# An FFN down-projection on one core: its first group's raw weights in buffers of another tag, and its residual loads ahead of the second group's operands

## The chip, the core and the metric

The kernel runs on one core of one Trainium2 chip. The metric is the device time of an execution in microseconds (us). PE is TensorE, DVE is VectorE, ACT is ScalarE, POOL is GpSimd; SP is the sync engine, which does nothing here but issue DMAs. GpSimd issues DMAs too, from a queue of its own.

## What is computed

One layer of a hybrid encoder, in float32, for two sequences of 512 tokens (called s0 and s1 in the kernel) of width 1024. Cut to what matters here:

```python
def encoder_layer(h, p, ...):
    ...                                   # pooling mixer and attention
    h = h + jnp.concatenate([y_pool, y_att], axis=-1) @ w_o
    u2 = rms_norm(h, ln2)
    h = h + (jax.nn.silu(u2 @ w_gate) * (u2 @ w_up)) @ w_down      # 1024 -> 2816 -> 1024
    gate = jax.nn.sigmoid(rms_norm(h, ple_norm) @ w_ple_gate)
    return h + gate * (p @ w_ple_proj)                             # p: 256 wide
```

## The kernel before, in words

Every product of matrices is made of three TensorE products: each operand is split into a high and a low part (L128 on ACT makes the high part, L131 on DVE the low one), and high x high, high x low and low x high are summed (L155 to L157).

**Seven products for eight.** From the FFN on, a block of two by two tiles is computed by a scheme of the Strassen-Winograd kind, in `seven` (L679 on): seven products where eight would be plain. Their moving operands are B11, B21, T1, T2, T4, T3, B22 (blocks of the activations, or sums of them); the block's rows are two feature tiles, its columns the two sequences. Each of the seven has its own stationary operand, which the generator `stationary` makes out of two raw weight tiles: three parts are pieces of the raw tiles, four are totals s1 to s4 (L641 on DVE), and all are split into high and low. These weights come from a ring W of 8 buffers, so they are made up to eight products ahead. The raw tiles are read by `load` (L139 to L142) from SP's queue into tag R, which has two buffers of 1024 columns. The product T2 is accumulated onto the PSUM bank of the product B11 after that has been read, T3 onto the same bank, and B22 onto the bank of T1.

**FFN up.** Eleven steps (two feature tiles each) make gate and up, then silu(gate) * up, and the seven operands of the down-projection. `spill` (L842 to L846) splits each and writes it to DRAM from SP's queue, through buffers `st` of tag V or, except in the last step, A.

**FFN down.** The 22 feature tiles are taken in groups of `DOWN = (2, 3, 3, 3)` pairs. A group reads its 7 n operand tiles (n is 2 or 3, 512 KB each) back from DRAM (L917, GpSimd's queue), into buffers whose tags come from the list `free`: TAGS of the seven names before (L723: PT, QK, A, A, A, QK, A). Then it runs four sevens (m = 0, 2, 4, 6 in L918 on), one per pair of output tiles; each is 7 x n x 3 matmuls of 128x512. Each product is added to the residual h by DVE in `got` (L929), eight additions a seven. Raw weight tiles of the first group have 512 columns (256 KB), those of the others 768.

**The residual h** has been saved to DRAM (hsave0 for s0, hsave1 for s1) before the FFN. It is read again in `h_again` (L890 to L894), two tiles of 512 KB (one of each sequence) ahead of each of the first group's four sevens, from GpSimd's queue: by `"VA"[q is s0]` s0's go into tag A and s1's into V. V has four buffers, which the last step's spills use until their DMAs have landed.

**After the down-projection** come the embedding products (e, `embed`, L942 on, from pT and w_pp, loaded by `embedding_operands` into tag A in the middle of the last group), a norm, and the last gate.

The order of the instructions on each engine is set by a scheduler from dependences and the order in which the program is written; buffers of a tag rotate, and whoever takes one waits until its last user is done. SP and GpSimd issue strictly in order, so a DMA that waits holds up all behind it. Buffers by tag: A 20, QK 8, V 4, PT 4, W 8, R 2, F 12 (of 512 columns, used for the FFN's intermediate x tiles), G 4.

Of the kernel before, what the change touches and what calls it, by code (L numbers as in the profile page):

```python
# [11 lines left out]
F32 = mybir.dt.float32  # L12
# [5 lines left out]
P = 128  # L18
T = 512
NT = T // P  # L20
D = 1024
KD = D // P
# [14 lines left out]
DOWN = (2, 3, 3, 3)  # L37
# [49 lines left out]
def hybrid_layer(ctx: ExitStack, tc: tile.TileContext, a: dict, out: bass.AP):  # L87
    nc = tc.nc
# [5 lines left out]
    def nm(s):  # L94
        serial[0] += 1
        return f"{s}{serial[0]}"

    def sbuf(s, tag, shape, dt):
        return pool.tile([P] + shape, dt, tag=tag, name=nm(s), bufs=BUFS[tag])

    def At(s, tag="A", dt=F32R):
        return sbuf(s, tag, [2, T], dt)

    def Ft(s):
        return sbuf(s, "F", [T], F32)
# [6 lines left out]
    def eng(name, i=0):  # L112

        return nc.gpsimd if TURNS[name][i % len(TURNS[name])] == "p" else nc.vector
# [10 lines left out]
    def split(hi, lo, src, hi_eng="act", lo_eng=nc.vector):  # L125

        if hi_eng == "act":
            nc.scalar.activation(hi, src, AF.Copy)  # L128
        else:
            nc.vector.tensor_copy(hi, src)  # L130
        lo_eng.tensor_tensor(lo, src, hi.bitcast(F32), op=ALU.subtract)  # L131
# [5 lines left out]
                                       op0=ALU.mult, op1=ALU.subtract)  # L137

    def load(src, n=D, tag="R"):  # L139
        raw = sbuf("raw", tag, [D], F32)  # L140
        nc.sync.dma_start(raw[:, :n], src)
        return raw  # L142

    def weight(src, n=D, tag="W", hi="act", lo=None, raw_tag="R"):
        raw = load(src, n, raw_tag)
        if lo is None:
            turn[1] += 1
            lo = eng(phase[0], turn[1])
        w = [sbuf("wh", tag, [D], F32R), sbuf("wl", tag, [D], F32R)]
        split(w[0][:, :n], w[1][:, :n], raw[:, :n], hi, lo)  # L150
        return w
# [76 lines left out]
    def square_sum(acc, x, first, eng):  # L228
        if first:
            nc.scalar.activation(acc, x, AF.Square)  # L230
        else:
            sq = Ft("sq")
            nc.scalar.activation(sq, x, AF.Square)
            eng.tensor_tensor(acc, acc, sq, op=ALU.add)
# [5 lines left out]
    seqs = [Seq(), Seq()]  # L240
    s0, s1 = seqs
# [125 lines left out]
    def pooling():  # L367
        for q in seqs:
            q.yp = []
            q.ypt = [At("yp", dt=F32) for _ in range(NG // 2)]  # L370
        raw = load(a["w_pool"], NG * P)
        wp = (sbuf("wp", "F", [T], F32R), sbuf("wp", "F", [T], F32R))
        split(wp[0], wp[1], raw[:, :NG * P], lo_eng=nc.gpsimd)
# [215 lines left out]
    def output(q, htag, bank):  # L589
        while len(q.ys) < KD:  # L590
            mixed(q, len(q.ys))
            if len(q.ys) % 4 == 0:
                yield
        q.h, q.hp = [], []
        q.sq = Ft("sqh")
        for m in range(KD):
            w = weight(a["w_o"][m])
            if m % 2 == 0:
                hp = At("h", htag, F32)
                nc.sync.dma_start(hp, a["xT"][q.s, :, m:m + 2, :])  # L600
                q.hp.append(hp)
            ps = Ps("o", bank)
            for i, (k, y) in enumerate(q.ys):
                mm3(ps, cols(w, k * P), act(y), i == 0, i == KD - 1)
                if i == KD // 2 - 1:
                    yield
            hm = hp[:, m % 2, :]
            nc.vector.tensor_tensor(hm, hm, ps, op=ALU.add)
            q.h.append(hm)
            square_sum(q.sq, hm, m == 0, eng("sqh", m))  # L610
            yield
# [14 lines left out]
        e.tensor_tensor(d, x, y, op=ALU.subtract)  # L626
        return d

    def stationary(srcs, n, part):


        half = n * P

        def parts(x, k):
            w = sbuf("w", "W", [2, T], F32R)
            split(w[:, 0, :half], w[:, 1, :half], x, lo_eng=eng("wlo", k))
            return w

        def total(x, y, op, k):
            d = sbuf("s", "G", [T], F32)[:, :half]  # L640
            eng("wadd", k).tensor_tensor(d, x, y, op=op)  # L641
            return d

        raw = load(srcs[0], 2 * half)
        a11, a12 = raw[:, :half], raw[:, half:2 * half]
        if part != 1:
            yield parts(a11, 0)
            yield parts(a12, 1)
        if part == 0:
            return  # L650
        raw = load(srcs[1], 2 * half)
        a21, a22 = raw[:, :half], raw[:, half:2 * half]
        s1 = total(a21, a22, ALU.add, 0)
        yield parts(s1, 2)
        s2 = total(s1, a11, ALU.subtract, 1)
        yield parts(s2, 3)
        yield parts(a22, 6)
        s3 = total(a11, a21, ALU.subtract, 3)
        yield parts(s3, 5)
        s4 = total(a12, s2, ALU.subtract, 2)  # L660
        yield parts(s4, 4)

    AHEAD = BUFS["W"]
    made, jobs = [], []
# [14 lines left out]
    def seven(u, n, got, a_tag=None, tags=(None,)):  # L679


        def product(ps, b, first):
            w = made.pop(0)
            for j in range(n):
                mm3(ps, (w[:, 0, j * P:(j + 1) * P], w[:, 1, j * P:(j + 1) * P]), act(b[j]), first and j == 0, j == n - 1,
                    not first)
            fill()
            return ps

        def bank(name):  # L690
            t = tags[turn[0] % len(tags)]
            if t is not None:
                turn[0] += 1
            return Ps(name, t)

        a = product(Ps("a", a_tag), u["B11"], True)
        got(0, a)
        got(1, product(bank("c"), u["B21"], True))
        yield
        b = product(bank("b"), u["T1"], True)  # L700
        got(2, b)
        got(3, product(a, u["T2"], False))
        got(4, product(bank("d"), u["T4"], True))
        got(5, product(a, u["T3"], False))
        got(6, product(b, u["B22"], False))
# [17 lines left out]
    TAGS = {"B11": "PT", "B21": "QK", "T1": "A", "T2": "A", "B22": "A", "T4": "QK", "T3": "A"}  # L723
# [11 lines left out]
    HALF = KD // 2  # L735
# [32 lines left out]
    def run(*gens):  # L768
        for g in gens:
            for _ in g:  # L770
                pass
# [14 lines left out]
    s0, s1 = seqs  # L786
# [29 lines left out]
    last = output(s1, "V", None)  # L816
    steps(last, 10)
    u = {}
# [8 lines left out]
    f0 = 0  # L827
    for n in DOWN:
        f1 = f0 + 2 * n
        jobs += [([a["w_down"][m + i, :, f0 * P:f1 * P] for i in range(2)], n, None) for m in range(0, KD, 2)]  # L830
        f0 = f1
    jobs += [(w, HALF, 0) for w in pg] + [(w, HALF, 1) for w in pg]
    fill()
# [5 lines left out]
    hsave = [[dram.tile([P, 2, T], F32, name=f"hsave{s}p{j}") for j in range(HALF)] for s in range(2)]  # L839
# [46 lines left out]
    for gg, gu in pairs:  # L886
        run(started.pop(0) if started else seven(u, HALF, gg))
        run(started.pop(0) if started else seven(u, HALF, gu))

    def h_again(j):  # L890
        for q in seqs:
            hp = At("h", "VA"[q is s0], F32)
            nc.gpsimd.dma_start(hp, hsave[q.s][j])
            q.h[2 * j:2 * j + 2] = [hp[:, 0, :], hp[:, 1, :]]  # L894


    def embedding_operands():
        wpp = [weight(a["w_pp"][f], tag="A", raw_tag="A") for f in range(2)]
        for q in seqs:
            raw = load(a["pT"][q.s], tag="A")  # L900
            pT = sbuf("pT", "A", [D], F32R), sbuf("pT", "A", [D], F32R)
            split(pT[0], pT[1], raw)
            q.pT = [cols(pT, f * T, T) for f in range(2)]
        return wpp


    free = [TAGS[k] for k in ORDER for _ in range(HALF)]
    f0 = 0
    for n in DOWN:
        f1 = f0 + 2 * n  # L910
        u = {}
        taken = [free.pop(0) for _ in range(len(ORDER) * n)]
        free += taken
        for i, k in enumerate(ORDER):
            u[k] = [At("u", taken[i * n + j]) for j in range(n)]
            for j, d in enumerate(u[k]):
                nc.gpsimd.dma_start(d.bitcast(F32), spilled[k][f0 // 2 + j])  # L917
        for m in range(0, KD, 2):  # L918
            if f1 == NF and m == EMB[2]:
                wpp = embedding_operands()  # L920

            if f0 == 0:
                h_again(m // 2)

            def got(i, ps, m=m):
                for h, k in ((s0.h[m], 0), (s0.h[m], 1), (s1.h[m + 1], 2), (s1.h[m], 3), (s0.h[m + 1], 4),
                             (s0.h[m + 1], 5), (s1.h[m + 1], 5), (s1.h[m], 6)):
                    if i == k:
                        nc.vector.tensor_tensor(h, h, ps, op=ALU.add)  # L929

            run(seven(u, n, got))
            if f1 == NF:
                for q in seqs:
                    if m == 0:
                        q.sq = Ft("sqp")
                    for i in range(2):
                        square_sum(q.sq, q.h[m + i], m + i == 0, eng("sqp", m + i))
        f0 = f1
# [16 lines left out]
    u = {}  # L955
# [117 lines left out]
```

## Time and profile before

| | us |
|---|---|
| median of 3 runs (lowest to highest) | 1203.9 (1200.99 to 1204.89) |
| the profiled execution's own time | 1204.31 |
| its span, first to last instruction | 1202.5 |
| PE busy in the span | 1137.3 (95%) |
| DVE busy | 926.4 (77%) |
| ACT busy | 592.2 (49%) |
| POOL busy | 241.3 (20%) |
| mean granted TensorE clock | 0.976 of full speed |

The profile is one execution. It has views of the whole (busy time by engine, the chain of work that ended last, groups of like instructions) and of stretches (timelines of an engine, waits, busy time by window, DMA issues). An entry such as `[8.07 <-ACT w L128]` says that the engine stood 8.07 us before this instruction, and that the last thing it waited for was an ACT instruction of line 128 that writes w. A DMA's row on SP or POOL is its issue, not its transfer. Consecutive DVE instructions overlap a little in the records, so the step from start to start is shorter than the duration.

### The profile page before, as it was taken

To read this page: it belongs to the slowest core of one execution; us is meant where nothing else is said; L and a number is where in the kernel's file an instruction comes from. 1 tells how busy PE (TensorE), PEld (TensorE's weight loads), DVE (VectorE), ACT (ScalarE), POOL (GpSimd) and SP (SyncE) were. 2 spreads that over 40 slices of the span, in tenths; PEclk is the share of its full clock that TensorE was granted. 3 is DMA by queue.
4 is the path that set the end of the run, shared out by engine and by line. 5 is a ranking of instruction groups with operands and counts; after the bars stand their busy time and mean duration, and the time that the engine had idled before them with its cause. 6 is when DMAs were issued, how large, how long until landed. Compare 5 with 4: busy or idle time off the path is not lost.

```text
span 1202.5 us, 15165 instructions
## 1 busy us (share of the span) xinstructions
PE 1137.3 (95%) x5232; PEld 938.9 (78%) x5232; DVE 926.4 (77%) x1738; ACT 592.2 (49%) x1135; POOL 241.3 (20%) x276
## 2 busy tenths in 40 slices
PE   8999989996999989999999999999969999999897
PEld 8898767784888867888888888888748888887675
DVE  7377889999774789987767877677658768884798
ACT  7154468777663535654545454455312222444553
POOL 3533553746240220000000000001312122001200
PEclk9899989998999999999999999999979999999999
DMA  6211100102233431554335442456978395626036
GB/s 215 69 56 55 38 1 1 53 15 74 88 108 121 140 105 53 196 189 175 122 124 192 152 177 100 150 193 236 404 289 321 120 352 183 250 66 210 26 122 220
DMA packets 53646, 173.28 MB, mean 144 GB/s; under 512 B 6208, under 2 KB 6976, under 8 KB 53568
## 3 DMA queue, kind: packets, MB, share of 16 engines
q1 hardware_dynamic: 41328, 127.73, 31.3%
q0 software_dynamic: 12240, 44.57, 9.6%
q8 instruction: 41, 0.67, 0.2%
q14 instruction: 37, 0.30, 0.1%
HBM read 119.33 MB, written 52.95 MB: 143 GB/s over the span
## 4 chain that ended last, share of the span: by engine, by line
PE 74%; DVE 14%; issue 5%; DMA 3%; POOL 2%; ACT 2%; SPq 0%; POOLq 0%; DVEq 0%; ACTq 0%
PE a L156 7%; PE a L157 7%; PE a L155 7%; PE b L155 5%; PE b L156 5%; PE b L157 5%; PE d L157 2%; PE d L156 2%; PE d L155 2%; PE o L155 2%; PE o L156 2%; PE o L157 2%; PE c L155 2%; PE c L157 2%; PE c L156 2%
## 5 line engine op out<-in xcount | busy, mean ns | idle before, releaser
L155 PE MATMUL a<-u,w 128*128 128x512 f32 x444 | 171.6, 392 | 10.0 <-ACT w L128 9.4
L156 PE MATMUL a<-u,w 128*128 128x512 f32 x444 | 174.0, 392 | 0.6 <-DVE u L131 0.3
L157 PE MATMUL a<-u,w 128*128 128x512 f32 x444 | 171.8, 391 | 1.0 <-DVE w L131 1.0
L128 ACT ACTIVATE w<-s 128x512 fp32r<-128x512 f32 (+2 forms) x168 | 97.2, 579 | 150.2 <-PE b L157 49.5
L128 ACT ACTIVATE w<-raw 128x512 fp32r<-128x512 f32 (+2 forms) x126 | 71.0, 577 | 172.2 <-PE a L157 98.1
L155 PE MATMUL b<-u,w 128*128 128x512 f32 x296 | 116.3, 394 | 6.8 <-DVE h L929 6.1
L131 DVE TENSOR_TENSOR w<-s,w 128x512 fp32r<-128x512 f32 (+2 forms) x168 | 104.2, 622 | 23.3 <-ACT w L128 22.6
L156 PE MATMUL b<-u,w 128*128 128x512 f32 x296 | 115.8, 392 | 3.7 <-DVE u L131 3.7
L157 PE MATMUL b<-u,w 128*128 128x512 f32 x296 | 116.0, 392 | 1.1 <-DVE w L131 1.1
L155 PEld LDWEIGHTS a<-u,w 128*128 128x128 f32 x444 | 83.8, 189 | 29.5 <-ACT w L128 10.6
L131 DVE TENSOR_TENSOR w<-raw,w 128x512 fp32r<-128x512 f32 (+2 forms) x126 | 78.4, 635 | 30.7 <-ACT w L128 30.7
L156 PEld LDWEIGHTS a<-u,w 128*128 128x128 f32 x444 | 83.8, 189 | 19.5 <-DVE u L131 1.5
L157 PEld LDWEIGHTS a<-u,w 128*128 128x128 f32 x444 | 83.8, 189 | 19.2 <-DVE w L131 1.9
L917 POOL DMA_DIRECT2D u<-opT4p x11 | 6.2, 563 | 414.8 <-DVE s L641 363.0
L155 PEld LDWEIGHTS b<-u,w 128*128 128x128 f32 x296 | 56.1, 189 | 20.2 <-DVE h L929 6.5
L156 PEld LDWEIGHTS b<-u,w 128*128 128x128 f32 x296 | 55.8, 189 | 16.6 <-DVE u L131 5.1
L157 PEld LDWEIGHTS b<-u,w 128*128 128x128 f32 x296 | 55.8, 189 | 13.4 <-DVE w L131 1.9
L155 PE MATMUL c<-u,w 128*128 128x512 f32 x148 | 58.9, 401 | 5.2 <-DVE x L727 5.2
L157 PE MATMUL c<-u,w 128*128 128x512 f32 x148 | 58.9, 398 | 0.0
L156 PE MATMUL c<-u,w 128*128 128x512 f32 x148 | 58.8, 397 | 0.0
L131 POOL TENSOR_TENSOR wl<-raw,wh 128x1024 fp32r<-128x1024 f32 (+4 forms) x24 | 50.2, 2095 | 37.1 <-ACT wh L128 32.8
L157 PE MATMUL d<-u,w 128*128 128x512 f32 x148 | 57.6, 389 | 0.0
(243 smaller groups left out, 2858.3 us busy)
## 6 DMA issues: line engine op xcount, KB each, us to landing
raw<-in_w_gate SPq DMA_DIRECT2D x24, 512.0 KB, 4.2
raw<-in_w_up SPq DMA_DIRECT2D x24, 512.0 KB, 3.6
raw<-in_w_down SPq DMA_DIRECT2D x24, 384.0 KB, 3.8
raw<-in_w_o SPq DMA_DIRECT2D x16, 512.0 KB, 3.6
raw<-in_w_pg SPq DMA_DIRECT2D x12, 512.0 KB, 3.7
opB11p<-st SPq DMA_DIRECT2D x11, 512.0 KB, 2.6
opB21p<-st SPq DMA_DIRECT2D x11, 512.0 KB, 3.7
opT1p<-st SPq DMA_DIRECT2D x11, 512.0 KB, 4.3
```

The source lines that it names most:

```text
L128: nc.scalar.activation(hi, src, AF.Copy)
L131: lo_eng.tensor_tensor(lo, src, hi.bitcast(F32), op=ALU.subtract)
L155: nc.tensor.matmul(ps, lhs[0], rhs[0], start=first, stop=False, skip_group_check=more)
L156: nc.tensor.matmul(ps, lhs[0], rhs[1], start=False, stop=False, skip_group_check=more)
L157: nc.tensor.matmul(ps, lhs[1], rhs[0], start=False, stop=last, skip_group_check=more)
L917: nc.gpsimd.dma_start(d.bitcast(F32), spilled[k][f0 // 2 + j])
```

## The change

1. `load` can use tag F, with 512 columns, and `stationary` takes the tag of its raw tiles. The first group's w_down tiles (512 columns) use F in place of R.
2. All h tiles go to tag A. They are loaded right behind the first group's operands, all eight in a row, s0 and s1 in turn.
3. The second and later groups' operand loads are written under `tc.issue_after(back.ins)`, where `back` is the last of the h loads: the scheduler puts them behind it in GpSimd's queue.
4. B22 gets the tag V in the list of tags that the groups take their operand buffers from.

```diff
     def load(src, n=D, tag="R"):
-        raw = sbuf("raw", tag, [D], F32)
+        raw = sbuf("raw", tag, [T if tag == "F" else D], F32)
...
-    def stationary(srcs, n, part):
+    def stationary(srcs, n, part, raw_tag="R"):
...
-        raw = load(srcs[0], 2 * half)
+        raw = load(srcs[0], 2 * half, raw_tag)
...
-        raw = load(srcs[1], 2 * half)
+        raw = load(srcs[1], 2 * half, raw_tag)
...
-        jobs += [([a["w_down"][m + i, :, f0 * P:f1 * P] for i in range(2)], n, None) for m in range(0, KD, 2)]
+        jobs += [([a["w_down"][m + i, :, f0 * P:f1 * P] for i in range(2)], n, None, "R" if f0 else "F") for m in range(0, KD, 2)]
...
+    for q in seqs:
+        q.h = [None] * KD
+
     def h_again(j):
         for q in seqs:
-            hp = At("h", "VA"[q is s0], F32)
-            nc.gpsimd.dma_start(hp, hsave[q.s][j])
+            hp = At("h", "A", F32)
+            last = nc.gpsimd.dma_start(hp, hsave[q.s][j])
             q.h[2 * j:2 * j + 2] = [hp[:, 0, :], hp[:, 1, :]]
+        return last
...
+    TAGS["B22"] = "V"
     free = [TAGS[k] for k in ORDER for _ in range(HALF)]
-    f0 = 0
-    for n in DOWN:
-        f1 = f0 + 2 * n
+
+    def loaded(n, f0):
         u = {}
         taken = [free.pop(0) for _ in range(len(ORDER) * n)]
-        free += taken
+        free.extend(taken)
         for i, k in enumerate(ORDER):
             u[k] = [At("u", taken[i * n + j]) for j in range(n)]
             for j, d in enumerate(u[k]):
                 nc.gpsimd.dma_start(d.bitcast(F32), spilled[k][f0 // 2 + j])
+        return u
+
+    f0 = 0
+    for n in DOWN:
+        f1 = f0 + 2 * n
+        if f0 == 0:
+            u = loaded(n, f0)
+            for j in range(HALF):
+                back = h_again(j)
+        else:
+            with tc.issue_after(back.ins):
+                u = loaded(n, f0)
         for m in range(0, KD, 2):
             if f1 == NF and m == EMB[2]:
                 wpp = embedding_operands()
-
-            if f0 == 0:
-                h_again(m // 2)
```

Where instructions stand now. On SP's queue, around the last step's spills (op... is a spill of that operand, raw a weight tile; a pair of raws feeds one seven). Before, the second pair's second raw, the spills, and the third pair:

```order
L141 DMA raw_7993<-in_w_down 128x512
L846 DMA opB11p_4441<-st_7911 128x1024
L141 DMA raw_8072<-in_w_down 128x512
L846 DMA opB21p_4452<-st_7972 128x1024
L846 DMA opB22p_4507<-st_7977 128x1024
L846 DMA opT1p_4463<-st_8002 128x1024
L846 DMA opT3p_4496<-st_8008 128x1024
L141 DMA raw_8135<-in_w_down 128x512
L141 DMA raw_8163<-in_w_down 128x512
```

With the change:

```order
L846 DMA opB11p_4441<-st_7911 128x1024
L141 DMA raw_7993<-in_w_down 128x512
L141 DMA raw_8084<-in_w_down 128x512
L141 DMA raw_8147<-in_w_down 128x512
L846 DMA opB21p_4452<-st_7972 128x1024
L141 DMA raw_8171<-in_w_down 128x512
L141 DMA raw_8234<-in_w_down 128x512
L846 DMA opB22p_4507<-st_7977 128x1024
L141 DMA raw_8258<-in_w_down 128x512
```

The third pair (8135 and 8163 before, 8147 and 8171 now) and the fourth (8234 and 8258 now) have moved from behind four spills to places in front of B22's spill or right behind it.

On GpSimd's queue, h of the second sequence and the second group's operands (u of T2, T4). Before:

```order
L917 DMA u_8433<-opT2p_4467 128x1024
L917 DMA u_8434<-opT2p_4468 128x1024
L917 DMA u_8438<-opT4p_4477 128x1024
L917 DMA u_8439<-opT4p_4478 128x1024
L893 DMA h_8052<-hsave1p_4512 128x1024
L893 DMA h_8143<-hsave1p_4513 128x1024
L893 DMA h_8234<-hsave1p_4514 128x1024
L893 DMA h_8325<-hsave1p_4515 128x1024
L917 DMA u_8440<-opT4p_4479 128x1024
```

With the change, from the first group's last operand on:

```order
L921 DMA u_8047<-opB22p_4498 128x1024
L896 DMA h_8050<-hsave0p_4508 128x1024
L896 DMA h_8052<-hsave1p_4512 128x1024
L896 DMA h_8054<-hsave0p_4509 128x1024
L896 DMA h_8056<-hsave1p_4513 128x1024
L896 DMA h_8058<-hsave0p_4510 128x1024
L896 DMA h_8060<-hsave1p_4514 128x1024
L896 DMA h_8062<-hsave0p_4511 128x1024
L896 DMA h_8064<-hsave1p_4515 128x1024
L921 DMA u_8416<-opB11p_4435 128x1024
```

Before, the four h loads of s0 stood behind the first group's operands, then 14 operand loads, then the four of s1. Now all eight stand together, and the operand loads follow.

On SP's queue near the end of the down-projection, the embedding inputs (pT) and the weights of the last gate (w_pg). Before:

```order
L141 DMA raw_9546<-in_w_down 128x768
L141 DMA raw_9654<-in_pT 128x1024
L141 DMA raw_9660<-in_pT 128x1024
L141 DMA raw_9624<-in_w_down 128x768
L141 DMA raw_9690<-in_w_down 128x768
L141 DMA raw_9768<-in_w_pg 128x1024
```

With the change:

```order
L141 DMA raw_9768<-in_w_pg 128x1024
L141 DMA raw_9810<-in_w_pg 128x1024
L141 DMA raw_9839<-in_w_pg 128x1024
L141 DMA raw_9654<-in_pT 128x1024
L141 DMA raw_9868<-in_w_pg 128x1024
L141 DMA raw_9660<-in_pT 128x1024
```

Both pT loads have moved behind the last w_down tiles and three or four of the w_pg tiles.

## Rows read from the trace of the kernel before

**Rows 1.** Of the kernel before, the page: busy time by engine (part 1) and the shares of the chain that ended last (part 4).

```profile
PE 1137.3 (95%) x5232; PEld 938.9 (78%) x5232; DVE 926.4 (77%) x1738; ACT 592.2 (49%) x1135; POOL 241.3 (20%) x276
...
PE 74%; DVE 14%; issue 5%; DMA 3%; POOL 2%; ACT 2%; SPq 0%; POOLq 0%; DVEq 0%; ACTq 0%
```

**Rows 2.** Of the kernel before, busy time by stretch, all engines. Columns: from:to and length in us; then PE, PEld, DVE, ACT and POOL busy us with the number of instructions; the granted TensorE clock as a share of full speed; the DMA engines' mean busy share; GB/s.

```profile
430.00:840.00 410.00, 402.82 (x1762) 331.47 (x1762) 321.13 (x521) 207.35 (x366) 5.90 (x9) 0.99 0.44 153
850.00:860.00 10.00, 10.00 (x46) 8.29 (x45) 7.56 (x14) 4.24 (x9) 3.78 (x7) 1.00 1.03 415
860.00:900.00 40.00, 25.34 (x93) 19.63 (x92) 23.86 (x52) 7.80 (x19) 7.02 (x13) 0.79 0.84 338
...
890.00:900.00 10.00, 8.60 (x30) 6.95 (x31) 9.34 (x20) 1.56 (x4) 0.00 (x0) 0.73 0.29 115
900.00:940.00 40.00, 40.00 (x178) 33.14 (x177) 33.56 (x65) 10.79 (x22) 7.55 (x14) 1.00 0.73 261
```

**Rows 3.** Of the kernel before, the timeline of PE between 875 and 897 us. Columns: start us, us, engine, line, operation, out<-in, count, and in brackets the idle time before it with what ended it.

```profile
877.58 0.79 PE L155 MATMUL a<-u,w 128*128 128x512 f32 x1 [8.07 <-ACT w L128]
...
891.40 0.80 PE L155 MATMUL b<-u,w 128*128 128x512 f32 x1 [6.13 <-DVE h L929]
...
895.40 0.39 PE L155 MATMUL a<-u,w 128*128 128x512 f32 x1
895.63 0.39 PE L156 MATMUL a<-u,w 128*128 128x512 f32 x1
```

**Rows 4.** Of the kernel before, the timeline of ACT (first row) and of DVE between 853 and 897 us, columns as in Rows 3.

```profile
877.11 0.72 ACT L128 ACTIVATE w<-raw 128x256 fp32r<-128x256 f32 x2 [4.83 <-DMA raw<-in_w_down]
...
855.18 1.28 DVE L717 TENSOR_TENSOR x<-x,a 128x512 f32<-128x512 f32 x2 [0.37 <-PE a L157]
...
861.27 0.68 DVE L929 TENSOR_TENSOR h<-h,a 128x512 f32<-128x512 f32 x1
861.87 0.68 DVE L929 TENSOR_TENSOR h<-h,d 128x512 f32<-128x512 f32 x1
...
864.60 0.41 DVE L641 TENSOR_TENSOR s<-s,raw 128x256 f32<-128x256 f32 x1
864.93 0.41 DVE L641 TENSOR_TENSOR s<-raw,raw 128x256 f32<-128x256 f32 x1
...
890.66 0.69 DVE L929 TENSOR_TENSOR h<-h,b 128x512 f32<-128x512 f32 x1 [8.23 <-DMA h<-hsave1p]
```

**Rows 5.** Of the kernel before, the timeline of SP's queue, which only issues DMAs; start us is when the DMA is issued, columns as in Rows 3.

```profile
847.97 0.33 SPq L141 DMA_DIRECT2D raw<-in_w_down  x1
859.57 0.32 SPq L846 DMA_DIRECT2D opB21p<-st  x1
...
866.64 1.00 SPq L141 DMA_DIRECT2D raw<-in_w_down  x2
...
873.03 0.33 SPq L846 DMA_DIRECT2D opT4p<-st  x1
881.12 1.66 SPq L141 DMA_DIRECT2D raw<-in_w_down  x2
```

**Rows 6.** Of the kernel before, the timeline of GpSimd's (POOL's) issued DMAs, columns as in Rows 3.

```profile
846.66 0.55 POOL L893 DMA_DIRECT2D h<-hsave0p  x1 [1.07 <-DMA u<-opB21p]
...
858.03 0.55 POOL L917 DMA_DIRECT2D u<-opB21p  x1 [0.72 <-PE c L157]
...
878.73 0.54 POOL L893 DMA_DIRECT2D h<-hsave1p  x1 [1.63 <-DVE w L131]
...
884.61 0.55 POOL L893 DMA_DIRECT2D h<-hsave1p  x1 [0.90 <-DMA u<-opT2p]
904.13 0.54 POOL L917 DMA_DIRECT2D u<-opT4p  x1 [18.98 <-PE a L157]
```

**Rows 7.** Of the kernel before, DMA issues between 825 and 905 us: out<-in, queue, count, size of one, median us from issue to landing.

```profile
h<-hsave0p POOLq DMA_DIRECT2D x4, 512.0 KB, 10.4
h<-hsave1p POOLq DMA_DIRECT2D x4, 512.0 KB, 10.4
raw<-in_w_down SPq DMA_DIRECT2D x7, 256.0 KB, 6.8
...
opT4p<-st SPq DMA_DIRECT2D x2, 512.0 KB, 9.5
```

**Rows 8.** Of the kernel before, groups of DVE instructions between 900 and 1000 us by shape: count, busy us and mean ns of one, idle before.

```profile
L929 DVE TENSOR_TENSOR h<-h,a 128x512 f32<-128x512 f32 x31 | 20.4, 681 | 9.0 <-PE a L157 9.0
L131 DVE TENSOR_TENSOR w<-s,w 128x384 fp32r<-128x384 f32 x27 | 14.9, 551 | 0.0
```

**Rows 9.** Of the kernel before, the end of the down-projection, in order: SP's timeline; one PE row of the timeline; the instructions that write or read the tile pT (min/median/max ns, first and last start); the DMA issues between 1030 and 1055 us.

```profile
1037.47 8.39 SPq L141 DMA_DIRECT2D raw<-in_pT  x2
...
1061.11 28.95 SPq L141 DMA_DIRECT2D raw<-in_w_pg  x6
...
1087.39 0.39 PE L157 MATMUL a<-u,w 128*128 128x512 f32 x1
...
L128 ACT ACTIVATE pT<-raw x2: 1047/1048/1050, 1042.2 to 1076.4; 128x1024 fp32r<-128x1024 f32 x2
L131 DVE TENSOR_TENSOR pT<-raw,pT x2: 1216/1218/1219, 1044.3 to 1078.5; 128x1024 fp32r<-128x1024 f32 x2
...
raw<-in_pT SPq DMA_DIRECT2D x2, 512.0 KB, 3.8
```

## The prediction

> **What bounds the kernel now.** Read the page first. TensorE (PE) is busy 95% of the span and carries 74% of the chain that ended last [rows 1], so only time in which PE stands, or runs slowly, can be won. Next I cut the span into stretches, to find such time [rows 2]: from 430 to 840 us PE is busy 402.82 of 410 us, from 900 to 940 all 40 us, at a granted clock of 0.99 and 1.00. Between 860 and 900 it is busy 25.34 of 40 us at a clock of 0.79. That stretch is the first group of the down-projection, the one the change touches. In matmuls: 178 fit in 40 us at full pace (0.2247 us each), 93 ran; the 85 missing are **19.1 us**, all that this place can give.
>
> PE's timeline says how they are lost [rows 3]. It stands 8.07 us before 877.58, released by ACT making a weight piece, and 6.13 us before 891.40, released by DVE's addition into h. Each time it then runs slowly: nine matmuls start from 891.40 until 895.40, where nine at full pace take 2.0 us: half the rate, the lower level of 1.2 GHz. The next step (895.40 to 895.63) is 0.23 again; 2.0 us are lost. With the same after the first stall, 8.07 + 6.13 + 4.0 = 18.2 of the 19.1 us.
>
> Then one step back from each releaser. ACT at 877.11 had waited 4.83 us for a raw weight, DVE at 890.66 had waited 8.23 us for h of the second sequence [rows 4]. Those are DMAs, so I read the queues. The third pair's two raws were issued by SP only at 866.64, just after DVE's totals at 864.60 and 864.93 had used the pair before [rows 4, 5]: tag R has two buffers. So they took 10.5 us to the ACT row, against a median of 6.8 [rows 7]. The second sequence's h was issued from 878.73 to 884.61, at the end of GpSimd's queue, behind 14 operand loads of the second group [rows 6], and took 10.4 us [rows 7]. Meanwhile the DMA engines are full: share 1.03 and 415 GB/s from 850 to 860, the mean still 0.84 to 900 [rows 2].
>
> **The change part by part.**
>
> *Raw weights in tag F.* No instruction is added: eight loads of 256 KB stay eight. Their issue no longer waits for R. They stand in front of or between the last spills; the third pair's second raw is right behind the B21 spill issued at 859.57, the fourth pair's last behind the next spill [rows 5]. With the longest landing seen, 10.5 us, the third pair is there at 859.9 + 10.5 = 870.4. PE starts the group near 855 and needs two sevens (42 matmuls, 9.4 us each) before the third pair, so not before 874. The first stall should go: 8.07 + 2.0 = 10.1 us. The second group's first two raws move up into old R slots; they are read later than before and nobody waits for them earlier.
>
> *h loads in tag A, eight in a row.* In the kernel before, GpSimd's eighth issue from 846.66 on is the one at 858.03 [rows 6]; the eighth h load takes that place. Plus 10.4 us [rows 7] gives 868.4, and some 2.2 us for 0.9 MB of raws that now go ahead of it at 415 GB/s: 870.6, 20 us before 890.66. The second sequence's first h stands second in the row: one seventh of the way from 846.66 to 858.03 is 848.3, plus 10.4 and 2.2 is 860.9, and DVE makes its first addition no earlier anyway (861.27) [rows 4]. The second stall should go too: 6.13 + 2.0 = 8.1 us.
>
> *Second group's operands behind h.* Four of the eight h loads, 2.1 MB, now precede them: 5.1 us at 415 GB/s. The first fourteen were through soon after 890, where the DMA share falls to 0.29 [rows 2]. With 5 us added by h and PE arriving 13 us earlier, at 893 to 899, the group's first three products find their data, and T2, the fourth, is needed 27 matmuls (6.1 us) later. The last seven loads waited 18.98 us, until 904.13, for PE to release their tiles [rows 6]; they go on being released by PE and move with it. I cost this at nothing; the cover is some 5 us, and a stall there would cost what it lasts, plus up to 2.0 us of slow running.
>
> A rule speaks against counting this as free. The Trainium skill, page "DMA: Bandwidth & Descriptors", section "Issuing engines are not separate DMA queues", says that DMAs started by different engines run on the same 16 DMA engines and interleave. The full DMA share in the trace agrees. By it the second stall would only be passed on to the operands that h overtakes, and the sum would be that of the second rival below.
>
> *What is late next: DVE.* From 855.18 to 861.27 it does nothing but the last FFN step [rows 4], 6.1 us, and has four more such pieces to do at 0.60 (the step from 861.27 to 861.87), 2.4. The group's 4 x 8 additions into h are 32 x 0.60 = 19.2. A pair of raws costs seven low parts and four totals: pieces of 256 columns step 0.33 (864.60 to 864.93), and three pairs are made in this stretch, since weights are eight ahead: 33 x 0.33 = 10.9. The second group's first pair is 11 pieces that last 0.55 [rows 8], some 0.08 less in steps, like the others: 5.2. Sum 43.8 us, against PE's 168 x 0.2247 = 37.8: six more than PE has. DVE may trail into the next group, where a seven gives PE 14.2 us and DVE 8 x 0.60 + 5.2 = 10.0. But T2's product accumulates on the bank from which h has just been taken, so DVE stands directly ahead of PE. Bounds 0 and 6.0; I take **5 us** as remaining loss, in stalls of 1 to 2 us, near the upper end because the backlog lies at the group's beginning. No row shows whether stalls that short cost clock; at most 2.0 each.
>
> *B22 and h tiles in other tags: the end of the down-projection.* Fewer A tiles are free there, so the embedding loads pT, issued at 1037.47 before, now wait until PE has read T2 and T4 of the last seven and stand between the w_pg loads in SP's queue. The embedding products, before mixed with the last down products (whose last starts at 1087.39), now all follow them [rows 9]. From the release to the first embedding product lie 30 matmuls, 6.7 us. Issue 0.33, landing 3.8, ACT 1.05 [rows 9] make 5.2; the low part, 1.22 on DVE, is needed three matmuls later, 6.4 against 7.4. That is 1 us of margin, with DVE's queue (pieces of 0.60) ahead of it. Bounds 0 and 4; I take **1 us**.
>
> Sum: 19.1 - 5 - 1 = 13.1 us won. The profiled execution took 1204.31 us around a span of 1202.5; 1204.3 - 13.1 = 1191.2. It stands 0.4 above the median of 1203.9, so I say **1191**.
>
> **The rivals.** A measurement of this kernel can tell 0.3%, 3.6 us, from no change: 1200.3 to 1207.5 counts as the same.
>
> 1. *All of it comes back.* DVE trails and PE never waits, pT is on time: 1203.9 - 19.1 = 1184.8. Against it: the 6 us of DVE work too much.
> 2. *Transfers keep one stall.* The second stall, or its like, moves to the second group's operands or to the first h: 19.1 - 8.1 - 5 - 1 = 5.0, so 1198.9. For it: the bytes are the same and the engines full until 890. Against it: what is overtaken is needed 10 us or more later.
> 3. *No net gain.* Raws late as well, say because SP's queue holds them behind spills: 10.1 stay, DVE takes 6, the tail 3: 19.1 - 19.1, so 1204.
> 4. *Slower: pT late in the tail.* One chain: w_pg raws in R release slowly, SP issues in order, pT stands behind them, PE waits with the embedding products. The six w_pg loads went out over 28.95 us from 1061.11 [rows 9]. Every us past the margin costs one, plus 2.0 of slow running. With the 14 us won before the tail, it decides from 14 + 3.6 - 2 = 15.6 us past the margin on; halfway along those 28.95 us it would be there only if pT waited for w_pg loads that stand behind it. At 20 us late: 1203.9 - 14 + 22 = 1212. If the first group gives only 5, 7 us late are enough.
>
> **How the numbers follow.** Forecast, 1186 to 1195: 0.52. First rival 0.08, second 0.21, third 0.11, fourth 0.08. The first two rivals and the forecast are faster by over 0.3%: 0.81; same 0.11; slower 0.08. The range leaves out the third and fourth, 0.19: from 1184.5 (first rival) to 1201 (upper end of the second).
>
> **What would show it.** Right: between 860 and 900 PE has over 150 matmuls and a clock near 1; no stall of PE over 3 us there; the waits of ACT for raw and of DVE for the second h are gone; what is left is PE waiting for DVE's h. DVE is busy over 90% there. At the end, PE waits under 2 us for pT. Wrong: a PE wait that goes back to an operand load between 890 and 915 (rival 2), to a raw before 880 (rival 3), or to pT (rival 4).

## The result and the profile after

The changed kernel takes **1190.46 us** (median of 4 runs, 1187.84 to 1192.21) against 1202.69 for the kernel before (4 runs in the same comparison); the ratio is 0.9897, with a 95% interval of 0.9875 to 0.9919. The forecast was 1191 us, with a range from 1184.5 to 1201. The profiled execution took 1191.35 us around a span of 1189.6, 13.0 less than the one before; the sum had said 13.1. By the medians the gain is 12.2 us, by the ratio 12.4, with 9.7 to 15.0 in its interval.

First the stretches of the first group again, in the changed kernel (columns as in [rows 2]):

```profile
850.00:860.00 10.00, 9.33 (x42) 7.39 (x40) 6.45 (x12) 2.82 (x6) 3.24 (x6) 1.00 1.03 406
860.00:900.00 40.00, 36.97 (x147) 29.61 (x148) 37.64 (x79) 12.68 (x31) 12.95 (x24) 0.91 1.03 412
...
900.00:940.00 40.00, 39.20 (x173) 31.99 (x172) 29.31 (x55) 9.18 (x19) 2.17 (x4) 1.00 0.50 179
```

147 matmuls stand where 93 stood [rows 2]; DVE is busy 37.64 of 40 us where it was 23.86; the DMA engines are full to the end (1.03, 412 GB/s) where their mean was 0.84: the gap in the transfers before 900 (0.29 from 890 to 900 in [rows 2]) is gone.

PE's timeline, the rows that answer to [rows 3]: the stalls that are left, and the first and last of the slow steps behind them.

```profile
861.24 0.50 PE L155 MATMUL a<-u,w 128*128 128x512 f32 x1 [1.90 <-DVE h L942]
...
861.82 0.52 PE L157 MATMUL a<-u,w 128*128 128x512 f32 x1
...
865.54 0.40 PE L155 MATMUL b<-u,w 128*128 128x512 f32 x1
...
871.82 0.50 PE L155 MATMUL b<-u,w 128*128 128x512 f32 x1 [1.80 <-ACT w L128]
...
875.80 0.40 PE L157 MATMUL a<-u,w 128*128 128x512 f32 x1
...
919.19 0.50 PE L155 MATMUL a<-u,w 128*128 128x512 f32 x1 [0.80 <-ACT w L128]
```

8.07 and 6.13 us have become 1.90, 1.80 and 0.80. From 861.82 to 865.54 nine matmuls start, which at full pace take 2.0 us: 1.7 lost. Eight start from 872.15 to 875.53, where 1.8 would do: 1.6 lost. Together 4.5 of idling and 3.3 of slow clock, 7.8 us.

DVE's timeline shows whom PE waits for (answers to [rows 4]):

```profile
860.50 0.68 DVE L942 TENSOR_TENSOR h<-h,a 128x512 f32<-128x512 f32 x1
861.10 0.69 DVE L131 TENSOR_TENSOR st<-td,st 128x512 fp32r<-128x512 f32 x1
...
866.43 0.69 DVE L942 TENSOR_TENSOR h<-h,b 128x512 f32<-128x512 f32 x1 [0.98 <-PE b L157]
868.25 1.88 DVE L942 TENSOR_TENSOR h<-h,a 128x512 f32<-128x512 f32 x3 [1.12 <-PE a L157]
870.23 0.69 DVE L942 TENSOR_TENSOR h<-h,c 128x512 f32<-128x512 f32 x1
870.84 0.42 DVE L641 TENSOR_TENSOR s<-raw 128x256 f32<-128x256 f32 x1
```

The first addition into h comes at 860.50, behind the last FFN step's pieces; PE's 1.90 us ends with it. The second pair's totals start at 870.84, behind additions for which DVE itself has waited for PE (0.98 and 1.12 us): PE's 1.80 us. So the second looks like an order and not an amount of work; an experiment below tries it.

The queues, SP first, then GpSimd (answer to [rows 5, 6]):

```profile
843.71 4.84 SPq L141 DMA_DIRECT2D raw<-in_w_down  x3
858.21 0.33 SPq L846 DMA_DIRECT2D opB21p<-st  x1
858.62 0.91 SPq L141 DMA_DIRECT2D raw<-in_w_down  x2
...
860.38 0.51 SPq L141 DMA_DIRECT2D raw<-in_w_down  x1
```

```profile
847.15 0.55 POOL L896 DMA_DIRECT2D h<-hsave0p  x1 [0.74 <-DMA u<-opB21p]
849.01 0.54 POOL L896 DMA_DIRECT2D h<-hsave1p  x1 [1.31 <-PE b L156]
...
859.30 0.55 POOL L896 DMA_DIRECT2D h<-hsave1p  x1 [0.75 <-issue]
...
888.41 0.54 POOL L921 DMA_DIRECT2D u<-opT4p  x1 [5.05 <-PE a L157]
```

The first group's raws left SP by 860.9 and the last h load left GpSimd at 859.30, against 882.8 (881.12 + 1.66 in [rows 5]) and 884.61. Of the second group's loads the last nine (T4, T3, B22) stand behind a wait of 5.05 us for PE's release; before it was the last seven, and 18.98 us. They come sooner as PE does.

### The profile page after: what moved, and what is told of

Its sections match the earlier page's. It is cut to its first block, busy times and chain, and to the rows that moved or that the text cites. A ratio compares the mean times of both kernels' runs of the same rounds, so it can differ in the third digit from the quotient of the medians.

```text
span 1189.6 us, 15167 instructions
## 1 busy us (share of the span) xinstructions
PE 1134.8 (95%) x5232; PEld 939.1 (79%) x5232; DVE 926.8 (78%) x1738; ACT 589.6 (50%) x1135; POOL 242.4 (20%) x276
## 4 chain that ended last, share of the span: by engine, by line
PE 79%; DVE 12%; issue 3%; ACT 2%; DMA 2%; POOL 1%; SPq 0%; DVEq 0%; ACTq 0%; POOLq 0%
PE a L156 8%; PE a L155 8%; PE a L157 8%; PE b L155 6%; PE b L156 6%; PE b L157 6%; PE d L155 3%; PE d L157 3%; PE d L156 3%; PE o L155 2%; PE o L156 2%; PE o L157 2%; PE c L155 2%; PE c L156 2%; PE c L157 2%
## 5 line engine op out<-in xcount | busy, mean ns | idle before, releaser
L156 PE MATMUL b<-u,w 128*128 128x512 f32 x296 | 117.6, 398 | 4.0 <-DVE u L131 4.0
L155 PE MATMUL b<-u,w 128*128 128x512 f32 x296 | 117.2, 397 | 2.9 <-ACT w L128 2.1
L157 PE MATMUL b<-u,w 128*128 128x512 f32 x296 | 117.1, 396 | 0.0
L155 PEld LDWEIGHTS b<-u,w 128*128 128x128 f32 x296 | 56.7, 192 | 17.0 <-ACT w L128 2.9
L156 PEld LDWEIGHTS b<-u,w 128*128 128x128 f32 x296 | 56.5, 191 | 17.0 <-DVE u L131 5.3
L157 PEld LDWEIGHTS b<-u,w 128*128 128x128 f32 x296 | 57.0, 193 | 12.1 <-DVE w L131 0.2
L942 DVE TENSOR_TENSOR h<-h,a 128x512 f32<-128x512 f32 x64 | 42.2, 683 | 25.4 <-PE a L157 25.3
```

Source lines behind the costliest of these rows:

```text
L155: nc.tensor.matmul(ps, lhs[0], rhs[0], start=first, stop=False, skip_group_check=more)
L156: nc.tensor.matmul(ps, lhs[0], rhs[1], start=False, stop=False, skip_group_check=more)
L157: nc.tensor.matmul(ps, lhs[1], rhs[0], start=False, stop=last, skip_group_check=more)
```

## The experiments

**Each half alone.** The first kernel is the one before with the raw weights' part only:

```diff
-        raw = sbuf("raw", tag, [D], F32)
+        raw = sbuf("raw", tag, [T if tag == "F" else D], F32)
...
-... n, None) for m in range(0, KD, 2)]
+... n, None, "R" if f0 else "F") for m in range(0, KD, 2)]
```

> The kernel before with the first part of the change alone: the first group's raw weights in tag F; h stays in its old place. Theory (the two waits lie over each other, the later one, h of the second sequence landing near 891, sets the time): the 8.1 us stall on a weight goes, but PE then stands before the same T1 or B22 product until about 891; one stall of 12 to 18 us in place of two, 0 to 3 us won (one phase of slow clock less): 1200 to 1204 us, 0.998 to 1.000 of before. Rival (each stall is worth what its row shows, 8.1 plus 2.0): 10 us won, 1193 us.

Measured: ratio 1.0028, interval 1.0010 to 1.0046 (1205.73 us). It gains nothing, and loses a little: just above the 1200 to 1204 expected, with the one stall in its 12 to 18. The waits of PE (engine, line and what it waited for: us in all, times, longest):

```profile
PE b L155 <- DVE h L929: 13.6, 1, 13.6
...
PE a L155 <- DVE h L929: 1.9, 1, 1.9
PE b L155 <- ACT w L128: 1.6, 1, 1.6
```

and the DVE addition that released it, with GpSimd's issue of that h:

```profile
891.95 0.69 DVE L929 TENSOR_TENSOR h<-h,b 128x512 f32<-128x512 f32 x1 [11.34 <-DMA h<-hsave1p]
```

```profile
882.09 0.54 POOL L893 DMA_DIRECT2D h<-hsave1p  x1 [0.99 <-issue]
```

PE reaches the same product earlier, and stands there until the same transfer has landed. The addition that waits for it starts 1.3 us later than before (890.66 in [rows 4]). What is new ahead of that transfer are two raws of the second group: by 891 us SP had issued eight raws of 256 KB in the kernel before, and here these eight and two of 384 KB, which find R free. Their 0.79 MB take 1.9 us at 415 GB/s. That they are the reason fits, but was not tried. The stall on weights had lain inside the wait for h: taking it away made the other longer.

The second kernel is the change with the first group's raws in R again (`"R" if f0 else "F"` becomes `"R"`):

> The change without its first part: the first group's raw weights in tag R again; h, the operand loads behind it and B22's tag as in the change. Theory (waits lie over each other): PE waits for the third pair's raws, issued only near 866 and landing near 877, and perhaps a second time for the fourth pair's, 8 to 12 us of stall in all with slow clock behind each; 4 to 8 us won of the 13: 1195 to 1199 us. Rival (each stall worth its row): the h stall's 8.1 us less 1 to 5 for DVE, 1195 to 1201, but then the weight stall must be 8 us as before and this and the run with the raws alone must add up to the change's 12 to 13 us. By the theory they add up to no more than 9.

Measured: 0.9919, 0.9897 to 0.9942 (1194.59 us), 9.7 us of 1203.2. PE's two rows with stalls:

```profile
877.07 0.79 PE L155 MATMUL a<-u,w 128*128 128x512 f32 x1 [3.72 <-ACT w L128]
...
900.23 0.79 PE L155 MATMUL a<-u,w 128*128 128x512 f32 x1 [3.74 <-ACT w L128]
```

Both end with a weight piece for which a raw was late (the second is of the second group, whose first raws also wait for R). So the halves alone give -3.4 and 9.7 us, 6.3 together, and both parts at once 12.4 (1 - 0.9897, of 1203). They do not add up, as the theory said (no more than 9). By the medians the raws' part is worth some 2.7 us beside h's, though the two intervals overlap, and less than nothing without it. The time of this second kernel alone would not decide: it lies just under both forecasts (from 1195 on). Its stalls (7.5 us, not 8 to 12) were less than expected.

**Is the rest DVE's order, or its amount?** In the change, the first group's additions from the sixth product of a seven on are put behind the next pair's totals:

```diff
-            eng("wadd", k).tensor_tensor(d, x, y, op=op)
+            totals.append(eng("wadd", k).tensor_tensor(d, x, y, op=op))
...
+                        last = made0 + 2 * m + (3 if i >= 5 else -1)
+                        if f0 == 0 and last >= made0:
+                            with tc.issue_after(totals[last].ins):
+                                nc.vector.tensor_tensor(h, h, ps, op=ALU.add)
```

> The change, and in the first group each addition into h from the sixth product of a seven to the fifth of the next is put behind the next pair's four totals in DVE's order. Theory (what is left of the group's loss is DVE's order, and a stall of under 2 us costs slow clock as well): the 1.80 us stall near 872 goes with the slow matmuls behind it, 3 to 4 us won against the change, 1186 to 1188 us. Rival (DVE simply has too much work in this stretch): the stall moves to another product, 1189 to 1192.

Measured: 0.9876, 0.9859 to 0.9893 (1188.38 us), 2.1 us less than the change by the medians, where 3 to 4 were expected. The 1.80 us stall is gone, with its slow matmuls:

```profile
860.00:900.00 40.00, 38.24 (x161) 31.36 (x162) 38.82 (x82) 12.60 (x31) 13.13 (x25) 0.96 1.03 412
900.00:940.00 40.00, 38.46 (x170) 31.52 (x169) 29.56 (x55) 9.74 (x20) 2.91 (x6) 1.00 0.56 200
```

161 matmuls in place of 147 are 3.1 us; 0.7 go again after 900, in a stall of 1.54 us on a low part. The profile shows the gain: from SP's issue of a spill ahead of the group to the last embedding product (two marks that are used again below) lie 270.2 us (823.51 to 1093.7), in the change 272.2. The intervals of the two ratios overlap, so the timed runs alone don't show it.

**Taking work off DVE, into GpSimd's queue.** The run before, with the last FFN step's two differences on GpSimd:

```diff
-            t1 = difference(x, x11, eng("hadd", 0))
+            t1 = difference(x, x11, eng("hadd", 0) if f + 2 < NF else nc.gpsimd)
...
-            t3 = difference(x22, x, eng("hadd", 1))
+            t3 = difference(x22, x, eng("hadd", 1) if f + 2 < NF else nc.gpsimd)
```

> The run before, and the last FFN step's two differences (td for T1 and T3) are made by GpSimd in place of DVE, so that the first addition into h comes ahead of T1's and T3's splits on DVE. Theory: the 1.90 us stall near 861 and its slow matmuls go too, 6 to 8 us won against the change, 1182 to 1185 us. Rival: GpSimd's differences hold up the DMA issues behind them in its queue, h or operands land later and PE waits for these: 1187 to 1195.

Measured: 0.9971, 0.9956 to 0.9985 (1199.01 us): the rival, and worse than it said. GpSimd's rows:

```profile
876.30 0.54 POOL L922 DMA_DIRECT2D u<-opT2p  x1 [0.74 <-issue]
876.85 2.49 POOL L626 TENSOR_TENSOR td<-x,x 128x512 f32<-128x512 f32 x2
899.67 0.58 POOL L922 DMA_DIRECT2D u<-opT4p  x1 [20.32 <-PE a L157]
```

Not DMAs stood behind the differences, but the differences behind ten operand loads, each of which is issued 1.3 to 2.5 us after the one ahead. In DVE's in-order queue their splits stood ahead of the second pair's totals, so DVE idled 16.11 us and PE 14.93:

```profile
878.82 1.08 DVE L131 TENSOR_TENSOR st<-td,st 128x512 fp32r<-128x512 f32 x1 [16.11 <-ACT st L128]
```

One thing did come as the theory said. With the differences and their splits out of the way DVE makes the first addition as soon as h has landed, and PE's 1.90 us are 0.43; the clock from 860 to 870 stays at 1.00:

```profile
858.90 0.69 DVE L949 TENSOR_TENSOR h<-h,a 128x512 f32<-128x512 f32 x1 [0.24 <-DMA h<-hsave0p]
...
859.64 0.50 PE L155 MATMUL a<-u,w 128*128 128x512 f32 x1 [0.43 <-DVE h L949]
```

So that stall, too, comes from what stands ahead of one instruction in DVE's queue.

Then the same with the differences between the sixth and seventh h load (`issue_after` of the last h pair on them), and T1's and T3's splits behind the first addition into h (T2's and T4's differences and splits then follow behind the second pair's totals):

```diff
+                t1, t3 = difference(x, x11, nc.gpsimd), difference(x22, x, nc.gpsimd)
+                deferred.append(late(j, x21, x22, t1, t3))
...
+                    with tc.issue_after(made_td[-1].ins), tc.issue_after(made_td[-2].ins):
+                        back = h_again(j)
```

> The run with the totals first, and the last FFN step's two differences on GpSimd again, but now in GpSimd's queue between the sixth and the seventh h load, where their inputs are ready (near 857.5), and T1's and T3's splits on DVE put behind the first addition into h. Theory (the 14.9 us stall of the run before was GpSimd's queue: td stood behind ten operand loads): that stall is gone; the first addition into h is made when h has landed, near 859, the stall near 861 is under 1 us and costs no clock; 3 to 4 us less than the run with the totals alone: 1184 to 1186 us. Rival: DVE's amount of work decides and the time stays at 1187 to 1190; or the last h pair, now 2.8 us later in the queue, is waited for: over 1190.

Measured: 0.9861, 0.9841 to 0.9880 (1187.79 us): in the rival's 1187 to 1190, not in the theory's 1184 to 1186. The 14.9 us are gone. The stall on the first addition did not fall under 1 us; it grew:

```profile
858.49 0.80 PE L155 MATMUL a<-u,w 128*128 128x512 f32 x1 [2.68 <-DVE h L973]
```

The rows of DVE and GpSimd show what held the addition:

```profile
854.58 3.26 DVE L131 TENSOR_TENSOR st<-x,st 128x512 fp32r<-128x512 f32 x1
857.76 0.68 DVE L973 TENSOR_TENSOR h<-h,a 128x512 f32<-128x512 f32 x1
...
854.77 2.51 POOL L628 TENSOR_TENSOR td<-x,x 128x512 f32<-128x512 f32 x2
```

DVE did not wait for h here. The split ahead of the addition lasted 3.26 us, where the like took 0.69 in the change, and GpSimd worked on its two differences in just that time, until 857.28. In the run before, the split that met the end of the differences took 1.08 in place of 0.69 as well (row 878.82). Both splits end 0.56 us after GpSimd's. As these two rows have it, moving the differences away from DVE held DVE up instead.

```profile
850.00:860.00 10.00, 7.32 (x30) 5.71 (x29) 9.97 (x13) 3.53 (x7) 6.22 (x9) 0.91 1.03 409
860.00:900.00 40.00, 39.88 (x174) 32.50 (x173) 38.43 (x82) 11.70 (x28) 12.59 (x25) 0.98 1.03 412
```

The 174 matmuls from 860 to 900 are no gain: this execution is 3.5 to 4.8 us ahead of the others at the first mark (819.40), so the stall and its slow steps lie before 860, where 30 matmuls stand for 44 in the run with the totals first. Between the marks it takes 270.0 us, as that run does (270.2). Whether DVE's amount of work would bind with both stalls gone, no run shows.

This and the run with the totals first are the fastest versions, both by their ratios faster than the kernel before; between them, and against the change, the intervals overlap.

**How much cover the overtaken operands have.** Copies of the saved h into a scratch tensor, read by nobody, between h and the second group's operands in the change:

```diff
+            for j in range(4):                       # 12 in the second kernel
+                with tc.issue_after(back.ins):
+                    back = nc.gpsimd.dma_start(scratch[j], hsave[j % 2][j // 2 % HALF])
```

> The change with four more transfers of 512 KB (a copy of the saved h to a scratch tensor in DRAM, read by nobody) in GpSimd's queue between the last h load and the second group's operands. At the 1.27 us that one takes while the engines are full, 5.1 us of traffic. Theory (the second group's operands have a cover of 5 us or more): 0 to 1 us more than the change, 1190 to 1192 us. Rival (DMA time is passed on whole): 4 to 6 us more, 1194 to 1197.

> The same with twelve such copies, 15.2 us of traffic. Theory (a cover of 6 us at the tightest operand, T4's second tile, landing near 902.6 and needed near 908): about 9 us of stall in the second group with up to 2 us of slow clock behind it: 1198 to 1203 us, PE waiting for an operand load between 890 and 925. Rival (DMA time is passed on whole): 1205 to 1208. Rival (the last operands are held by PE's release, not by the queue): 1190 to 1194.

Measured: 0.9875, 0.9857 to 0.9893 (1188.99 us) with four, 0.9961, 0.9947 to 0.9975 (1199.34 us) with twelve. Four cost nothing that the runs can tell. With twelve PE waits for operand loads, many times and briefly:

```profile
PE a L155 <- DMA u<-opT3p: 1.6, 3, 1.1
PE b L155 <- DMA u<-opT1p: 1.2, 1, 1.2
PE b L155 <- DMA u<-opB22p: 1.0, 3, 0.4
```

The mean clock from 900 to 940 is 0.96 in that kernel, with 129 matmuls for 173. The twelve are in the theory's range (1198 to 1203). A copy took longer than the 1.27 us put into the expectation: the twelve landed from 873.8 to 891.7, 1.6 us apart, with spills of SP's queue between them, so the four are an estimated 6.5 us of traffic and the twelve 19.5. Of these 19.5, 7.7 to 10.3 were paid (0.9961 against the change's 0.9897 and the four copies' 0.9875, of 1204 us), slow clock included. By this estimate the cover is some 9 to 12 us, nearly double what the prediction said.

One part was not tried alone: B22's tag.

## Why the prediction was right, and where it wasn't

*The time.* Right in direction and mechanism, and in number partly by luck: the sum's terms err on both sides. Two marks split it: SP's issue of one spill ahead of the group (B21 of the last step but one), and the last embedding product. Of the kernel before, then of the changed one (for the product: min/median/max ns, first and last start):

```profile
824.19 0.33 SPq L846 DMA_DIRECT2D opB21p<-st  x1
...
L157 PE MATMUL e<-pT,wl x32: 388/389/397, 1080.1 to 1107.2; 128*128 128x512 f32 x32
```

```profile
823.07 0.33 SPq L846 DMA_DIRECT2D opB21p<-st  x1
...
L157 PE MATMUL e<-pT,wl x32: 388/389/486, 1072.8 to 1095.3; 128*128 128x512 f32 x32
```

Between the marks 283.0 us became 272.2, so the group gave **10.8**. For this stretch the forecast was 14.1 (19.1 - 5) less the 1 us for a late pT, which would lie between the marks as well: 13.1. Behind the marks 95.3 became 94.3, a gain of 1.0 that was not forecast. Ahead of them 1.1 us differ where nothing was changed: scatter, since this mark lies between 822.9 and 824.2 in eight of the profiled executions, and at 819.4 in the ninth. So the profiled 12.9 us of span are 10.8 + 1.0 + 1.1, and only the first term is what the prediction spoke of.

*The two stalls, 10.1 and 8.1 us.* Each is gone, as forecast. But they were priced as two sums that add up, and that step was wrong: the runs with each half alone show the wait for weights inside the wait for h. What set the end was the landing of h; the raws matter only once h is early. The total did not suffer, as the change takes both waits away; the prices of rivals 2 and 3, which keep one of them, did.

*What is late next: DVE.* Right, and so was its place: the accumulating T2 product behind the addition into h, and an order of waits of 1 to 2 us. The term was mis-sized: 5 us taken, 8.3 lost (19.1 - 10.8), because 3.3 us of slow clock behind two stalls of under 2 us were bounded and then left at nothing. For the same reason two of the signs of being right were not met: 147 matmuls and a clock of 0.91 from 860 to 900, where over 150 and a clock near 1 were named (DVE's share, 94%, and the longest stall, 1.90 us, were as said). And "no row shows whether stalls that short cost clock" was not so. The kernel before has such a row earlier in its trace, in which PE ran on at full pace; at the same place in the changed kernel the stall is a little longer, and nine slow steps follow, 1.7 us:

```profile
457.04 0.50 PE L156 MATMUL b<-u,w 128*128 128x512 f32 x1 [1.61 <-DVE u L131]
```

```profile
454.95 0.50 PE L156 MATMUL b<-u,w 128*128 128x512 f32 x1 [1.90 <-DVE u L131]
```

The row before would have pointed to no cost, and so misled. The reason given for the term was half right: counting 43.8 us of DVE work against PE's 37.8 suggested an amount. The run with the totals first (161 matmuls, the 1.80 us gone) and the first run with GpSimd's differences (1.90 us down to 0.43) show that each of the two stalls hangs on the order on DVE; no run removed both.

*h and raws by the queues.* The last h load left at 859.30 (forecast 858.03), the last raw by 860.9, both well ahead of need. The first addition into h came at 860.50 (861.27).

*The second group's operands.* At no cost, as forecast; the cover was larger, by the copies. The rule of the Trainium skill (page "DMA: Bandwidth & Descriptors", section "Issuing engines are not separate DMA queues") fits what is seen: the engines' share is 1.03 as before, and in the run with the raws alone two more raws on SP's queue go with an h on GpSimd's that is 1.3 us later. That made rival 2 possible; the cover kept it away.

*The tail.* The pT loads did come late and just in time: the low part of pT starts on DVE at 1070.5 and lasts 1.22, so ends at 1071.7, where the first embedding product starts at 1071.94. PE never waits for it; the 1 us of cost didn't come. The margin is thin: in the run with the totals first PE waits 0.36 us for pT. The part behind the last embedding product is shorter in all kernels with h in tag A (93.1 to 94.3 us), and not in the one with raws alone (95.2), so it belongs to that half of the change. Of PE's waits there (the first three rows are of the kernel before, the last of the changed one), 2.9 us for weights became 0.3:

```profile
PE b L157 <- DVE w L131: 1.1, 1, 1.1
PE a L157 <- DVE w L131: 1.0, 2, 0.6
PE a L155 <- ACT w L128: 0.8, 1, 0.8
```

```profile
PE b L155 <- ACT w L128: 0.3, 1, 0.3
```

These are weights of the last gate; SP issued the first w_pg loads at 1050.18 and the last at 1081.79, against 1061.11 [rows 9] and 1096.32. Another wait of 0.7 us comes in, and the clock there is 0.96 in place of 0.98, which leaves 1.0. That the earlier loads are the cause was not tried.

*The rivals.* DVE trailing for free (rival 1) fell by the slow clock and the order; rivals 2, 3 and 4 by the rows above: PE's 1.90, 1.80 and 0.80 us go back to DVE, and no wait to an operand load, a raw or pT.

## What to carry to other kernels

Two stalls in a row on one engine are not two gains: before adding them up, ask when the later one would end if the earlier were gone; if a transfer's issue sets that, only the transfer's move is worth anything. A stall of just under 2 us on TensorE can cost nearly 4, and the second half shows only in the granted clock; a slightly shorter one cost no more than itself here. Work that is moved to an engine that issues DMAs stands in line with them: look at its place in that queue before at its duration, and at what the engine that was relieved does meanwhile.

## What the runs showed of the hardware

Stalls of 1.90 and 1.80 us were each followed by eight or nine matmuls at half pace (0.43 us a step, the lower level of 1.2 GHz; clock 0.83 in the ten us around each), so that the clock's part was nearly as large as the stall. Stalls of 1.61 us (the kernel before, at 457.04), 1.62 us (the run with the raws alone, at 869.27) and 1.54 us were followed by full pace; the last is in the run with the totals first:

```profile
913.05 0.50 PE L157 MATMUL a<-u,w 128*128 128x512 f32 x1 [1.54 <-DVE w L131]
```

While GpSimd made its differences a DVE split with two inputs stood: 3.26 us in place of 0.69 in one run, 1.08 in another, both ending 0.56 us after GpSimd.

Twelve copies of 512 KB from DRAM to DRAM, with spills between them, landed 1.6 us apart; from the first to the last landing the engines moved 367 GB/s, and in the same stretch of the change 415.
